# Five of ten down-weight pieces built behind the next tile's gate operands in a SwiGLU layer

## Chip, cores and metric

The kernel runs one whole transformer layer on one core of a Trainium2 chip, as one launch. The metric is device time in microseconds (us) of that launch, as the median of several runs. TensorE is called PE here (its weight loads PEld), VectorE DVE, ScalarE ACT, GpSimd POOL and SyncE SP; SP issues the DMA transfers that are spoken of below.

## What is computed

The layer has a mixer (a Fourier part and a retention part) and a SwiGLU channel mixer. The change is in the second one. Cut to it, the reference is:

```python
def swiglu(u, wg, wu, wd):
    return (jax.nn.silu(u @ wg) * (u @ wu)) @ wd

u2 = modulate(layer_norm(x), sh2, sc2)          # (1, 2048, 1024)
x = layer_norm(DEEPNORM_ALPHA * x + gt2 * swiglu(u2, w_ffn_gate[l], w_ffn_up[l], w_ffn_down[l]),
               ln2_g[l], ln2_b[l])              # gate, up: 1024 x 2816, down: 2816 x 1024
```

All of it is in float32. The kernel makes each float32 operand of a product into two float16 parts (high and low) and multiplies three pairs of them, so one product costs three passes of PE.

## The kernel before

**Tiles.** The 2816 hidden columns are cut into 22 blocks of 128, taken two at a time: `j` runs over `HJ` = 11 tiles, and for each `j` the loop `for gu` does the gate (`gu` = 0) and then the up projection (`gu` = 1). Below, G3 is the gate half of tile 3 and U3 its up half. Each half is one level of a Strassen scheme: seven products of half-size operands instead of eight, for each of the two halves of the sequence (`sb` 0 and 1). So a half is 14 products, and a product is 12 matmuls of 128x128 by 128x512 (`prod`, with the three passes of `mm3`, L152 to L154).

**PSUM banks.** A sequence half uses one bank `x` (`proj` for `sb` 0, `misc` for `sb` 1), into which A11, S2, S3 (and A22) are summed one onto the other, and one bank `z` (`s0`, `s1`) for S1 and S4. A12 has a bank of its own (`tq`, `zt`). After A11, S2 and S3 the present sum is copied out by ACT into a tile named `p`, `a` or `b` (`keep`, L1353). PE may add the next product onto `x` only when this copy is done. The order of the products in a half is A11 S1 (`sb` 0), A11 S1 (`sb` 1), S2, S2, then A12 S3, A12 S3, then A22 S4, A22 S4. `done` finishes a quarter: DVE adds (L1340 of the gate, L1347 and L1348 or L1344 of the up), ACT applies silu (L1338, L1341). After an up quarter, `h_part` makes sums of the hidden tile on POOL (L1306 to L1314), splits some in two with ACT and DVE (`half_split` into the tile `ht`, of which there is one, L1187 and L1188), and SP stores them.

**Operands.** For each half, SP loads two raw weight tiles (`w_raws`, L1104). `right` makes seven operands of them: POOL does four subtractions (L985, L987, L990, L992), and `split` makes the float16 parts into `ws` tiles, high on ACT (L148), low on DVE (L149). This runs one half ahead of PE.

**Down weights.** The second matrix product, with `w_ffn_down`, comes later and reads operands from DRAM. They are made in the loop over `j`, in ten pieces, `down(i, c)` with `i` from 0 to 4 and `c` 0 or 1; below D0 to D9 in the order of their issue. A piece loads two raw tiles in four transfers (L1199), has POOL scale them by the output gate (L1200) and form differences (L1213 to L1216 and L1225 to L1228, 24 instructions), has ACT and DVE split 17 groups of them into `wdo` tiles (L148, L149; there are two such tiles), and has SP store seven results (L1210, L1221). The eleventh tile has a different function, `down_last`.

**What sets the order.** Every engine runs its instructions in program order. The order within an engine comes from a scheduler that simulates the program when it is built; it takes the source order as priority and places an instruction of later source where an engine would stand idle in its simulation. Tiles come from pools by tag: three `raw` tiles are shared by gate, up and down weights, twelve `ws` tiles by operands and temporaries. So a piece's loads can only start when a raw tile of the stream ahead of it is free, and the next gate's or up's load only when the piece has let go of one.

In source order the program makes the operands of G0, U0, D0, G1, U1, D1, G2 and so on; with the half ahead, the work of D(n) in the trace lies beside PE's G(n).

Of the kernel before, what the change touches and what calls it, by code (L numbers as in the profile page):

```python
# [79 lines left out]
def layer_kernel(ctx: ExitStack, tc: tile.TileContext, a, out):  # L80
# [19 lines left out]
    def mk(pool, shape, dt=F32, tag=None, bufs=1):  # L100
        return pool.tile(shape, dt, name=nm(tag), tag=tag, bufs=bufs)
# [26 lines left out]
    def raw_tile(shape=(P, 2, 512), dt=F32):  # L128
        return mk(wp, list(shape), dt, tag="raw", bufs=3)

    def ws_tile(shape=(P, 2, 512), dt=F16):
        return mk(wp, list(shape), dt, tag="ws", bufs=12)
# [14 lines left out]
    def split(hi, lo, raw, scale=SW):  # L147
        S.activation(hi, raw, AF.Copy, scale=scale)  # L148
        V.scalar_tensor_tensor(lo, raw, scale, hi, ALU.mult, ALU.subtract)  # L149
# [1024 lines left out]
    HP = HJ // 2  # L1174
# [15 lines left out]
    def down(i, c):  # L1190

        raws = []
        for half in range(2):
            raw = raw_tile((P, 2, 4, P))
            r0 = (2 * i + HJ * half) * P
            gv = gt2.rearrange("p (q n) -> p q n", q=4)[:, :, c * P : (c + 1) * P]
            for k in range(2):
                src = wd_in[r0 + k * P : r0 + (k + 1) * P].rearrange("p (q n) -> p q n", q=4)
                Q.dma_start(raw[:, k], src[:, :, c * P : (c + 1) * P])  # L1199
                G.tensor_tensor(raw[:, k], raw[:, k], gv, ALU.mult)  # L1200
            raws.append(raw)
        q0, q1 = raws[0][:, :, 0:2], raws[0][:, :, 2:4]
        q2, q3 = raws[1][:, :, 0:2], raws[1][:, :, 2:4]
        t1 = ws_tile((P, 2, 2, P), F32)

        def op(o, x):
            if o in ONE:
                w = mk(cq, [P, 2, 2, 2, P], F16, tag="wdo", bufs=2)
                split(w[:, :, 0], w[:, :, 1], x)
                Q.dma_start(wd_d[o][:, 2 * i : 2 * i + 2, c], w.rearrange("p k s y n -> p k s (y n)"))  # L1210
                return
            t = ws_tile((P, 4, P), F32)
            G.tensor_tensor(t[:, 3], x[:, 0, 1], x[:, 0, 0], ALU.subtract)  # L1213
            G.tensor_tensor(t[:, 0], x[:, 1, 1], t[:, 3], ALU.subtract)
            G.tensor_tensor(t[:, 1], x[:, 1, 1], x[:, 0, 1], ALU.subtract)
            G.tensor_tensor(t[:, 2], x[:, 1, 0], t[:, 0], ALU.subtract)  # L1216
            w = mk(cq, [P, 7, 2, P], F16, tag="wdo", bufs=2)
            split(w[:, 0:2, 0], w[:, 0:2, 1], x[:, :, 0])
            split(w[:, 2:6, 0], w[:, 2:6, 1], t)
            split(w[:, 6, 0], w[:, 6, 1], x[:, 1, 1])  # L1220
            Q.dma_start(wd_d[o][:, :, i, c], w)  # L1221

        op(0, q0)
        op(1, q2)
        G.tensor_tensor(q0, q1, q0, ALU.subtract)  # L1225
        G.tensor_tensor(t1, q3, q0, ALU.subtract)
        G.tensor_tensor(q1, q3, q1, ALU.subtract)
        G.tensor_tensor(q2, q2, t1, ALU.subtract)  # L1228
        for o, x in enumerate((t1, q1, q2, q0, q3)):
            op(2 + o, x)  # L1230
# [49 lines left out]
    for j in range(HJ):  # L1280
# [37 lines left out]
        for gu, src in enumerate((wg_in, wu_in)):  # L1318
# [44 lines left out]
            def product(o, sb, loose=False):  # L1363


                d = st[sb]
                if o == A11:
                    d["x"] = prod(w, o, sb, (("proj", "misc")[sb],))
                    keep(sb, "p", d["x"])
                elif o == A12:  # L1370
                    done(sb, 0, d["p"], prod(w, o, sb, (("tq", "zt")[sb],)))
                elif o == S2:
                    keep(sb, "a", prod(w, o, sb, None, d["x"]))
                elif o == S1:
                    d["z"] = prod(w, o, sb, (("s0", "s1")[sb],))
                elif o == S3:
                    keep(sb, "b", prod(w, o, sb, None, d["x"]))
                    done(sb, 3, d["b"], d["z"])
                elif o == A22 and loose:
                    done(sb, 2, d["b"], prod(w, o, sb, (("tq", "zt")[sb],)))  # L1380
                elif o == A22:
                    done(sb, 2, None, prod(w, o, sb, None, d["x"]))
                else:
                    done(sb, 1, d["a"], prod(w, o, sb, None, d["z"]))
# [18 lines left out]
            else:  # L1403

                for part in (ORDER[0:2], ORDER[2:3], ORDER[3:5], ORDER[5:7]):
                    for sb in range(2):
                        for o in part:
                            product(o, sb)
        if j < 2 * HP:
            down(j // 2, j % 2)  # L1410
    es_c.close()


# [103 lines left out]
    for o, sb in TWO:  # L1517
        hq, last = h_next
        n = TWO.index((o, sb)) + 1
# [163 lines left out]
```

## Time and profile before

| | |
|---|---|
| three runs | 2118.32 us median (2117.81 to 2122.67) |
| the profiled execution | 2121.23 us, of it a span of 2119.4 us |
| PE busy in the span | 2025.6 us (96%) |
| DVE busy | 1408.6 us (66%) |
| ACT busy | 795.0 us (38%) |
| POOL busy | 757.0 us (36%) |

The times in the trace are counted from the start of the span. The loop over `j` has its gate half G1 at about 993 us and then a half every 36.26 us where PE does not wait. In a row of a timeline, the two numbers ahead are start and duration; brackets give how long the engine stood idle before and what released it. A row of the waits gives the sum, the count and the longest. A row of the windows gives, after the stretch and its length, the busy time of PE, PEld, DVE, ACT and POOL with the number of instructions in brackets, then PE's granted clock, the DMA share and GB/s.

### The profile page before, as it was taken

What the parts mean: (1) busy time and instruction counts of PE and PEld (TensorE: products, weight loads), DVE (VectorE), ACT (ScalarE), POOL (GpSimd) and SP (SyncE); (2) the same over time, 40 slices, a digit from 0 to 9 for tenths busy, and PEclk for the clock granted to TensorE, in tenths of its full rate; (3) what the DMA queues carried; (4) which work ended last, traced back from release to release, by engine and by line L of the source; (5) the groups of instructions that cost most, each with busy time, mean ns of one, the idle gap of its engine ahead of it and who ended that gap; (6) DMA issues with size and microseconds to landing.
All of it is one profiled execution on the core that took longest, in us unless ns stands there. A gap on an engine that the chain in (4) does not pass through costs nothing.

```text
span 2119.4 us, 30963 instructions
## 1 busy us (share of the span) xinstructions
PE 2025.6 (96%) x11678; PEld 1178.6 (56%) x11678; DVE 1408.6 (66%) x2546; ACT 795.0 (38%) x1438; POOL 757.0 (36%) x800
## 2 busy tenths in 40 slices
PE   6999989999999899989899999999999999999997
PEld 5456676458557544444344444444444458888743
DVE  7976385757547577786566556656655558878676
ACT  5624432243233244463433443343334324333132
POOL 3322412221222136646675566556655500000010
PEclk9999999999999999999999999999999999999999
DMA  9531121332211545644434443444444369665652
GB/s 292 179 120 51 37 63 60 110 96 64 89 45 51 168 166 194 229 139 148 138 121 142 123 144 127 141 123 146 129 126 143 115 235 346 208 221 204 245 179 105
DMA packets 300342, 305.19 MB, mean 144 GB/s; under 512 B 15448, under 2 KB 248992, under 8 KB 299040
## 3 DMA queue, kind: packets, MB, share of 16 engines
q1 hardware_dynamic: 293376, 287.08, 42.3%
q10 hardware_dynamic: 6816, 16.12, 2.1%
q8 instruction: 92, 1.51, 0.3%
q14 instruction: 58, 0.48, 0.1%
HBM read 200.25 MB, written 102.90 MB: 143 GB/s over the span
## 4 chain that ended last, share of the span: by engine, by line
PE 57%; DVE 17%; DMA 9%; POOL 8%; ACT 4%; issue 3%; SPq 2%; POOLq 0%; DVEq 0%; ACTq 0%
PE proj L152 8%; PE proj L154 8%; PE proj L153 8%; PE misc L152 4%; PE misc L154 4%; PE misc L153 4%; PE s L152 3%; PE s L154 3%; PE s L153 3%; DMA raw<-in_w_mod_dram 3%; DVE raw L377 2%; DVE ws L149 2%; DMA raw<-in_w_ffn_down_dram 1%; DVE st L178 1%; POOL us L1088 1%
## 5 line engine op out<-in xcount | busy, mean ns | idle before, releaser
L152 PE MATMUL proj<-ws,uhi 128*128 128x512 f16 (+1 forms) x768 | 251.2, 327 | 4.2 <-ACT sg L774 3.2
L154 PE MATMUL proj<-ws,ulo 128*128 128x512 f16 (+1 forms) x768 | 251.1, 327 | 0.0
L153 PE MATMUL proj<-ws,uhi 128*128 128x512 f16 (+1 forms) x768 | 251.0, 327 | 0.0
L153 PEld LDWEIGHTS <-ws 128*128 128x128 f16 x1296 | 127.8, 99 | 172.7 <-issue 25.4
L152 PEld LDWEIGHTS <-ws 128*128 128x128 f16 x1296 | 127.7, 99 | 155.8 <-issue 6.8
L154 PEld LDWEIGHTS <-ws 128*128 128x128 f16 x1296 | 127.4, 98 | 153.6 <-issue 3.2
L167 POOL TENSOR_TENSOR rstd<-ve,mhalf 128x1 f32<-128x1 f32 x66 | 38.9, 599 | 455.6 <-DVE ve L165 444.0
L149 DVE SCALAR_TENSOR_TENSOR ws<-raw,ws 128x512 f16<-128x512 f32 x186 | 146.0, 800 | 62.8 <-ACT ws L148 61.0
L148 ACT ACTIVATE ws<-raw 128x512 f16<-128x512 f32 x186 | 114.0, 626 | 89.1 <-POOL raw L992 40.8
L1187 ACT CAST ho<-h 128x1280 f16<-128x1280 f32 x70 | 87.4, 1258 | 151.9 <-DVE h L1440 35.7
L149 DVE SCALAR_TENSOR_TENSOR wdo<-raw,wdo 128x256 f16<-128x256 f32 (+1 forms) x100 | 66.5, 687 | 109.1 <-ACT wdo L148 109.1
L152 PE MATMUL proj<-u2b,ws 128*128 128x512 f16 x344 | 130.8, 380 | 8.4 <-ACT a L1353 4.0
L152 PE MATMUL misc<-u2a,ws 128*128 128x512 f16 x344 | 130.2, 379 | 6.6 <-ACT p L1353 4.7
L154 PE MATMUL proj<-u2b,ws 128*128 128x512 f16 x344 | 131.1, 381 | 0.0
L153 PE MATMUL proj<-u2b,ws 128*128 128x512 f16 x344 | 130.9, 380 | 0.0
L153 PE MATMUL misc<-u2a,ws 128*128 128x512 f16 x344 | 130.4, 379 | 0.1
L154 PE MATMUL misc<-u2a,ws 128*128 128x512 f16 x344 | 130.4, 379 | 0.0
L1188 DVE TENSOR_TENSOR ho<-h,ho 128x1280 f16<-128x1280 f32 x70 | 103.9, 1489 | 20.2 <-ACT ho L1187 20.1
L153 PEld LDWEIGHTS <-uhi 128*128 128x128 f16 x768 | 75.5, 98 | 46.9 <-issue 5.3
L154 PEld LDWEIGHTS <-ulo 128*128 128x128 f16 x768 | 75.6, 98 | 44.8
L152 PEld LDWEIGHTS <-uhi 128*128 128x128 f16 x768 | 76.0, 99 | 42.9 <-issue 1.3
L149 DVE SCALAR_TENSOR_TENSOR wdo<-ws,wdo 128x512 f16<-128x512 f32 (+2 forms) x70 | 58.7, 861 | 50.4 <-ACT wdo L148 49.4
(493 smaller groups left out, 5304.5 us busy)
## 6 DMA issues: line engine op xcount, KB each, us to landing
h<-h SPq DMA_DIRECT2D x40, 640.0 KB
raw<-in_w_mod_dram SPq DMA_DIRECT2D x88, 256.0 KB
wd<-wdo SPq DMA_DIRECT2D x50, 448.0 KB
wd<-wd SPq DMA_DIRECT2D x33, 640.0 KB
h<-sg SPq DMA_DIRECT2D x60, 256.0 KB
raw<-in_w_ffn_gate_dram SPq DMA_DIRECT2D x22, 512.0 KB
raw<-in_w_ffn_up_dram SPq DMA_DIRECT2D x22, 512.0 KB
raw<-in_w_ffn_down_dram SPq DMA_DIRECT2D x40, 256.0 KB
```

The costliest lines, as they stand in the source:

```text
L148: S.activation(hi, raw, AF.Copy, scale=scale)
L149: V.scalar_tensor_tensor(lo, raw, scale, hi, ALU.mult, ALU.subtract)
L152: T.matmul(o, sh, mh, start=first, stop=False, skip_group_check=onto)
L153: T.matmul(o, sh, ml, start=False, stop=False, skip_group_check=onto)
L154: T.matmul(o, sl, mh, start=False, stop=last, skip_group_check=onto)
L167: pows.append(G.tensor_tensor(rstd, ve, mhalf[:, 0:n], ALU.pow).ins)
L178: V.bn_stats(st[:, hf], xt[:, hf * 512 : hf * 512 + 512])
L377: V.scalar_tensor_tensor(r[0], r[k], sil[:, v, k : k + 1], r[0], ALU.mult, ALU.add)
L1088: (V if o in (2, 5) or (sb and i >= 2 and o != 4) else G).tensor_tensor(dst[:, :, 1], src, dst[:, :, 0], ALU.subtract)
L1187: S.copy(dst[:, 0], src)
L1188: V.tensor_tensor(dst[:, 1], src, dst[:, 0], ALU.subtract)
```

## The change

The call of `down` goes into the loop over gate and up. Piece n = j - 1 of the first five is issued behind the gate of tile j, so behind the gate that follows its old place; pieces five to nine stay behind the up of their own tile.

```diff
@@ -1406,8 +1406,10 @@
                     for sb in range(2):
                         for o in part:
                             product(o, sb)
-        if j < 2 * HP:
-            down(j // 2, j % 2)
+
+            n = j - 1 if gu == 0 else j
+            if (gu == 0 and 0 <= n < HP) or (gu == 1 and HP <= n < 2 * HP):
+                down(n // 2, n % 2)
     es_c.close()
```

The source order was U0 D0 G1 U1 D1 G2 U2 D2 G3 ... and is now U0 G1 D0 U1 G2 D1 U2 G3 D2 U3 G4 D3 U4 G5 D4 U5 D5 G6; from G6 on both are alike. No instruction is added or taken away in `down` itself.

The first place is POOL's order behind the operands of U0 (`ws_9737` is a temporary of theirs). Before, the four scalings L1200 of D0 (`raw_10005`, `raw_10010`) and its differences follow at once:

```order
L987 TENSOR_TENSOR ws_9737<-raw_9735,raw_9733 128x512
L1200 TENSOR_TENSOR raw_10005<-raw_10005,gt_9623 128x512 x2
L992 TENSOR_TENSOR raw_9735<-raw_9735,ws_9737 128x512
L1213 TENSOR_TENSOR ws_10016<-raw_10005 128x128
L1215 TENSOR_TENSOR ws_10016<-raw_10005 128x128
L1214 TENSOR_TENSOR ws_10016<-raw_10005,ws_10016 128x128
L1200 TENSOR_TENSOR raw_10010<-raw_10010,gt_9623 128x512
```

Now the operands of G1 (`raw_10007`, `raw_10009`, L985 to L992) come first, and D0 (now `raw_10237`, `raw_10242`) after and between them:

```order
L987 TENSOR_TENSOR ws_9737<-raw_9735,raw_9733 128x512
L992 TENSOR_TENSOR raw_9735<-raw_9735,ws_9737 128x512
L985 TENSOR_TENSOR raw_10007<-raw_10007 128x512
L1200 TENSOR_TENSOR raw_10237<-raw_10237,gt_9623 128x512
L990 TENSOR_TENSOR raw_10007<-raw_10009,raw_10007 128x512
L987 TENSOR_TENSOR ws_10011<-raw_10009,raw_10007 128x512
L1200 TENSOR_TENSOR raw_10237<-raw_10237,gt_9623 128x512
L992 TENSOR_TENSOR raw_10009<-raw_10009,ws_10011 128x512
L1200 TENSOR_TENSOR raw_10242<-raw_10242,gt_9623 128x512 x2
L1213 TENSOR_TENSOR ws_10248<-raw_10237 128x128
```

D0 has moved behind one whole set of operands, that of G1.

The second place is ACT's order while PE does G2. The tiles `p_`, `a_`, `b_` are the copies out of the banks `proj` and `misc`; the `wdo` rows are the first splits of a down piece, of its scaled raw tile. Before, they stand ahead of the copies `a`:

```order
L1187 CAST ht_10593<-sg_10094 128x512
L1353 COPY p_10758<-misc_10745 128x512
L148 ACTIVATE ws_10941<-raw_10919 128x512
L148 ACTIVATE wdo_11218<-raw_11194 128x2x128
L148 ACTIVATE wdo_11218<-raw_11194 128x128
L148 ACTIVATE ws_10944<-raw_10919 128x512
L1353 COPY a_10785<-proj_10717 128x512
L1353 COPY a_10799<-misc_10745 128x512
L148 ACTIVATE wdo_11205<-ws_11200 128x4x128
L1341 ACTIVATE sg_10685<-sg_10685 128x512
L1353 COPY b_10828<-proj_10717 128x512
```

Now the copies `a` come first, and the first splits of the down piece stand ahead of the copies `b`:

```order
L148 ACTIVATE ws_10937<-raw_10917 128x512
L148 ACTIVATE ws_10941<-raw_10919 128x512
L1187 CAST ht_10593<-sg_10006 128x512
L148 ACTIVATE ws_10944<-raw_10919 128x512
L1353 COPY a_10697<-proj_10629 128x512
L1353 COPY a_10711<-misc_10657 128x512
L148 ACTIVATE ws_11196<-raw_11191 128x512
L148 ACTIVATE wdo_11437<-raw_11421 128x2x128
L148 ACTIVATE wdo_11437<-raw_11421 128x128
L1341 ACTIVATE sg_10597<-sg_10597 128x512
L1353 COPY b_10740<-proj_10629 128x512
```

The wait for a piece's raw tile has moved from the copy of the second product onto `proj` to that of the third, and the splits of the up operands (`raw_10919`) stand among the rows ahead of `a`.

The third place is SP's order around the raw tiles of U2 (`raw_10917`, `raw_10919`). Before, both are loaded together, behind the last store of D1:

```order
L1221 DMA wd_9615<-wdo_10669 896x1x256
L1210 DMA wd_9616<-wdo_10677 128x2x512
L1104 DMA raw_10689<-in_w_ffn_gate_dram 128x8x128
L1210 DMA wd_9617<-wdo_10681 128x2x512
L1104 DMA raw_10917<-in_w_ffn_up_dram 128x8x128
L1104 DMA raw_10919<-in_w_ffn_up_dram 128x8x128
```

Now the second one stands alone, behind a store of D1 and stores of the hidden tile:

```order
L1293 DMA h_9584<-sg_10005 256x1x256
L1293 DMA h_9585<-hs_10522 256x1x256
L1210 DMA wd_9616<-wdo_10909 128x2x512
L1104 DMA raw_10919<-in_w_ffn_up_dram 128x8x128
L1221 DMA wd_9615<-wdo_10901 896x1x256
```

The first load `raw_10917` has stayed far ahead; the second one now follows the piece that holds the third raw tile.

## Prediction

> **What bounds the kernel now.** I read the page first, then the waits of PE, then the windows of the stretch that the change touches.
>
> ```profile
> span 2119.4 us, 30963 instructions
> PE 2025.6 (96%) x11678; PEld 1178.6 (56%) x11678; DVE 1408.6 (66%) x2546; ACT 795.0 (38%) x1438; POOL 757.0 (36%) x800
> ```
>
> PE is busy 96% of the span. The change gives PE no work and takes none, so it can only move PE's waits, and only where it moves instructions, from U0 to G5. The windows show this stretch by halves and tiles; the second number is the length, the third is PE's busy time.
>
> ```profile
> 937.90:975.10 37.20, 35.82 (x165) 15.99 (x165) 25.73 (x35) 20.18 (x42) 27.60 (x32) 1.00 0.28 79
> 975.10:992.80 17.70, 16.71 (x76) 7.42 (x76) 12.31 (x19) 6.66 (x12) 4.21 (x4) 1.00 0.65 193
> 1100.00:1172.00 72.00, 72.00 (x335) 32.59 (x333) 43.55 (x55) 27.63 (x55) 43.55 (x44) 1.00 0.44 133
> ```
>
> From 1100 us on PE is full: there is nothing to win there. What there is to win lies before it, and the waits of PE name it (from 940 to 1100 us, then from 1100 to 1690 us):
>
> ```profile
> PE misc L152 <- ACT p L1353: 3.6, 2, 3.3
> PE proj L152 <- ACT a L1353: 3.5, 2, 2.1
> PE s L152 <- DVE sg L1340: 1.3, 1, 1.3
> PE proj L152 <- ACT p L1353: 0.9, 1, 0.9
> PE s L152 <- DVE c L1347: 0.7, 1, 0.7
> PE misc L152 <- ACT b L1353: 0.3, 1, 0.3
> ```
>
> ```profile
> PE misc L152 <- ACT p L1353: 1.2, 3, 0.7
> PE proj L152 <- ACT a L1353: 0.6, 1, 0.6
> ```
>
> The first list sums to 10.3 us: U0 has 1.3 + 0.7 + 0.3 = 2.3, G2 has 0.3 + 1.3 = 1.6 (its parts of the first two rows), and G1 has the rest, 0.9 + 3.3 + 2.1 = 6.3. G1 also pays for a low clock right behind its longest wait:
>
> ```profile
> 1018.86:1022.27 3.41, 3.41 (x10) 1.20 (x9) 1.72 (x3) 1.15 (x2) 3.17 (x4) 0.50 0.21 77
> ```
>
> 3.41 us at a granted clock of 0.50 do the work of 1.7 us, so 1.7 us are lost and G1 costs 8.0 in all. **The stake is 2.3 + 8.0 + 1.6 = 11.9 us**, half a per cent of the time. After 1100 us all waits sum to 1.8 us, most of them in tiles that the change leaves alone.
>
> The waits of G1 come from ACT's queue, not from its load; here are its rows in that stretch:
>
> ```profile
> 1003.13 0.61 ACT L148 ACTIVATE wdo<-raw 128x256 f16<-128x256 f32 x2 [1.75 <-POOL raw L1200]
> 1003.66 0.57 ACT L1353 COPY p<-proj 128x512 f32<-128x512 f32 x1
> 1009.15 0.63 ACT L148 ACTIVATE ws<-raw 128x512 f16<-128x512 f32 x1 [4.93 <-POOL raw L992]
> 1009.69 0.57 ACT L1353 COPY p<-misc 128x512 f32<-128x512 f32 x1
> 1016.61 0.62 ACT L1187 CAST ht<-hs 128x512 f16<-128x512 f32 x1 [4.79 <-DMA h<-ht]
> 1017.14 0.58 ACT L1353 COPY a<-proj 128x512 f32<-128x512 f32 x1
> ```
>
> Each copy that PE wants stands behind an instruction that itself waits: for a down piece (L1200), for POOL's last operand of the next up half (L992), for the store of `ht`.
>
> **The change, part by part.** *U0.* D0's splits leave PE's way there. The add that PE waited for sat on DVE behind one of them:
>
> ```profile
> 974.02 0.43 DVE L149 SCALAR_TENSOR_TENSOR wdo<-raw,wdo 128x256 f16<-128x256 f32 x1 [1.32 <-ACT wdo L148]
> 974.36 0.68 DVE L1340 TENSOR_TENSOR sg<-a,s 128x512 f32<-128x512 f32 x1
> ```
>
> Of 2.3 I leave 0.5 (bounds 0 and 2.3): -1.8.
>
> *G1.* D1 no longer stands ahead of `p<-proj`, so the wait of 0.9 goes. L992 and the store of `ht` remain ahead of the next two copies, and D0, which now runs from U0's late products into G1, takes D1's place on POOL. Floor: two thirds of the 6.3 gone, 2. Ceiling: all as now, 8. The two waits left sum to 3.3 + 2.1 = 5.4; with a difference of D1 less ahead of each on POOL (0.46, the row of L1213 below) they come to 4.5, and the longer, 2.8, is shorter than the 3.3 behind which the low clock stood. I take 4.5: -3.5.
>
> *G2 to G4.* Here the change can lose. The present state, in G3, which begins at 1148.42 us:
>
> ```profile
> 1164.97 0.62 ACT L148 ACTIVATE wdo<-raw 128x256 f16<-128x256 f32 x2 [3.91 <-POOL raw L1200]
> 1165.49 0.61 ACT L148 ACTIVATE ws<-raw 128x512 f16<-128x512 f32 x1
> 1166.01 0.56 ACT L1353 COPY a<-proj 128x512 f32<-128x512 f32 x1
> ```
>
> ```profile
> 1161.37 0.38 PE L152 MATMUL misc<-u2a,ws 128*128 128x512 f16 x1
> 1163.96 0.38 PE L152 MATMUL tq<-u2b,ws 128*128 128x512 f16 x1
> 1166.62 0.38 PE L152 MATMUL proj<-u2b,ws 128*128 128x512 f16 x1
> ```
>
> A product takes 1163.96 - 1161.37 = 2.59 us. The copy ends at 1166.57, PE uses it at 1166.62: the slack of `a<-proj` is 0.05 us already. The order shows that the piece's first split moves from ahead of `a<-proj` (needed by the 8th product) to ahead of `b<-proj` (needed by the 11th), three products or 7.8 us later. But the piece is later too. I rebuild its chain from the durations of the old one:
>
> ```profile
> 1092.31 0.46 POOL L1213 TENSOR_TENSOR ws<-raw 128x128 f32<-128x128 f32 x1
> 1121.03 1.26 POOL L987 TENSOR_TENSOR ws<-raw,raw 128x512 f32<-128x512 f32 x1 [8.70 <-DMA raw<-in_w_ffn_gate_dram]
> 1162.44 2.49 POOL L1200 TENSOR_TENSOR raw<-raw,gt 128x512 f32<-128x512 f32 x2 [4.02 <-DMA raw<-in_w_ffn_down_dram]
> ```
>
> ```profile
> 1116.23 0.64 SPq L1104 DMA_DIRECT2D raw<-in_w_ffn_gate_dram  x1
> 1159.00 1.27 SPq L1199 DMA_DIRECT2D raw<-in_w_ffn_down_dram  x2
> ```
>
> ```profile
> 1129.11 0.69 DVE L149 SCALAR_TENSOR_TENSOR ws<-raw,ws 128x512 f16<-128x512 f32 x1 [0.71 <-ACT ws L148]
> ```
>
> From a piece's first L1213 to the load into the raw tile that it frees: 1116.23 - 1092.31 = 23.9. From that load to L987: 1121.03 - 1116.23 = 4.8. From L987 to the last split of the set: 1129.80 - 1121.03 = 8.8. From a down load to L1200: 1162.44 - 1159.00 = 3.4, and L1200 takes 2.5. In the new order a piece's L1213 needs a `ws` tile that the 6th product of the up half lets go: 6 x 2.59 = 15.5 us into it, or 20.7 us before the next gate. So, from the gate's start: second up load at +3.2, L987 at +8.0, last split and with it the next down loads at +16.8, L1200 at +20.2, done +22.7. Then ACT's `wdo` split (0.62) and DVE's part behind it with an add, a silu and the copy `b<-proj` (0.56, as `a`): some 3.7 in sum, so +26.4. PE needs it after ten products, at +25.9: **0.5 us late**, if nothing else holds the chain up.
>
> What may hold it up is that the piece now meets the up half's own DVE work. The up half has less of POOL's, the gate half more:
>
> ```profile
> 1112.16:1148.42 36.26, 36.26 (x169) 16.43 (x168) 20.39 (x28) 12.72 (x25) 14.73 (x12) 1.00 0.44 132
> 1148.42:1184.68 36.26, 36.26 (x169) 16.46 (x168) 23.17 (x28) 15.24 (x30) 28.98 (x33) 1.00 0.44 135
> ```
>
> so 14 us of POOL's time change halves and the load is evener, if anything. But a multiply of the up takes longer when POOL works (here beside L1308) than when it doesn't:
>
> ```profile
> 1137.60 0.69 DVE L1348 SCALAR_TENSOR_TENSOR sg<-c,sg 128x512 f32<-128x512 f32 x1
> 1146.90 1.75 DVE L1348 SCALAR_TENSOR_TENSOR sg<-c,sg 128x512 f32<-128x512 f32 x1
> ```
>
> That is 1.06 us each. Two such steps inside the chain, and sums of `h` between the piece's steps on POOL (1.3 to 1.7 us each), give a late copy of up to 4 to 5 us; nothing in the way gives 0. I take the value near the lower middle, 0.5 + 1.06 + about half a sum = 2 in each of G2, G3 and G4. The Trainium skill (SBUF — State Buffer, "Who interferes with whom") says that a DVE instruction with two SBUF inputs contends with a GpSimd instruction that reads SBUF, and that the loser waits for the whole instruction. The 1.75 against 0.69 agrees in kind; by that rule every multiply that meets a piece would pay, which speaks for the upper end and against the change, and the sum would be nearer 4 than 2 per gate.
>
> *G5.* The last moved piece, D4, is done in U5 and D5 follows at its old place, so `a<-misc` stands behind a later L1200: 0.6 to 3, taken as 2. *G6 on*: same order, nothing.
>
> *The DMAs.* A piece's four loads and seven stores move with it, on the same queue and in the same number; at a DMA share of 0.44 I give them nothing, and the second up load that slips behind them is in the chain above.
>
> **Sum.** Before 2.3 + 8.0 + 1.6 = 11.9. After 0.5 + 4.5 + 3 x 2 + 2 = 13.0. That is +1.1 on the profiled execution's 2121.2 us. The profile lies 2.9 us above the median of the runs, which is 2118.3, so I forecast **2119.4 us**: no change. A measurement of this kernel tells about 0.3%, 6.4 us, from none. With the small ends (0, 2, 0, 0, 0, 0.6) the sum is 2.6, with the large ones 2.3 + 8 + 3 x 4.5 + 3 = 26.8: from -9.3 to +14.9.
>
> **Rivals.**
> *A: the moved pieces fit.* The slack of three products is enough in G2 to G5 and only G1 keeps 2 to 3 us. For it: the load gets evener, and the chain above is late by 0.5 only. Against it: `a<-proj` and `p<-misc` had hardly any slack before. Sum 2.6 instead of 11.9: 2109.
> *B: the third product becomes the wait of every gate, slower.* `b<-proj` at 11 products, late by 4 to 5 us in each of G2 to G5, since multiplies and sums of `h` lengthen the piece; G1 as now, 8. It decides as soon as the chain grows by over 3 us from +26.4. From 3.3 us on, such a wait would bring the low clock too, 1.7 us each. 0.5 + 8 + 4 x 4.5 = 26.5, or +14.6: 2133; with the low clock four times 2140. The Trainium skill (TensorE: Matmul & The Clock Gate, Part 1, "What's actually happening") gives an idle window of about 3.4 us as what halves the clock; G1's low clock stood behind 3.28 us, and by that figure a wait of 2 stays free of it.
> *C: the change doesn't do what it says.* The `raw` and `ws` tiles hold a piece back anyway, so that it runs where it ran, and only the queues differ: within 2 us, 2118.
>
> **Chances.** Forecast 0.48, A 0.25, B 0.22, C 0.05. Most of A, all beyond -6.4, is faster: 0.24 with a bit of the forecast's lower side. B nearly all is slower, with some of the forecast's upper side: 0.25. The rest, 0.51, is within 0.3%. The range takes A's 2109 and B's 2133 as ends, without B's low clock; the likeliest case alone, 2113 to 2125.
>
> **What the profile after would show.** Right: the waits on `p` and `a` of G1 shrink to 4 to 5 us with no low clock; U0 loses its wait on `sg`; in G2 to G4 the waits name `b` with about 2 us, behind a `wdo` split released by L1200. A: no waits from 1045 us on. B: `b` with 4 us or more in each gate, and a granted clock under 1 in that stretch. Wrong in another way: waits that name PE's weights (`ws`), since then the second up load, not ACT's queue, would be what is late; or a wait in an up half, which I have as free.

## The result

| | before | after |
|---|---|---|
| median, us | 2120.49 (4 runs, 2117.81 to 2125.43) | 2147.15 (4 runs, 2142.49 to 2151.64) |
| ratio to before | | 1.0118, 95% interval 1.0096 to 1.0140 |
| span of the profiled execution, us | 2119.4 | 2147.9 |

The kernel became slower by 1.2%, some 25 us. The forecast was no change, and the time lies above the range that was given. The profile of the changed kernel answers to the first two lines shown in the prediction:

```profile
span 2147.9 us, 30963 instructions
PE 2033.2 (95%) x11678; PEld 1178.3 (55%) x11678; DVE 1421.7 (66%) x2546; ACT 798.7 (37%) x1438; POOL 767.9 (36%) x800
```

The same number of instructions is busy longer on PE (by 7.6 us) and on DVE (by 13.1 us). To see where the time came from, both executions are cut at the same points of the program: the first of the last seven products of G0, A12 onto `tq` in U1, and A12 onto `tq` in G6. The windows of the kernel before:

```profile
937.91:1053.12 115.21, 106.50 (x481) 47.31 (x480) 75.97 (x96) 51.31 (x103) 76.84 (x79) 0.99 0.43 127
1053.12:1381.65 328.53, 326.90 (x1514) 147.96 (x1512) 200.76 (x248) 122.24 (x240) 196.66 (x192) 1.00 0.44 134
```

and of the kernel after:

```profile
936.28:1045.83 109.55, 105.84 (x481) 47.20 (x481) 64.53 (x85) 47.44 (x92) 60.51 (x55) 0.98 0.35 103
1045.83:1406.64 360.81, 336.70 (x1514) 149.74 (x1513) 223.49 (x259) 129.39 (x250) 222.33 (x215) 0.98 0.43 131
```

The start (U0, G1 and the first part of U1) gained 115.21 - 109.55 = 5.7 us. The stretch of the moved pieces D1 to D4 behind it lost 360.81 - 328.53 = 32.3 us. Of the remaining program, the part ahead took 1.6 us less and the part behind 3.5 us more. Of the 32.3 us, 9.8 are the same 1514 matmuls taking longer (336.70 against 326.90). Some 8 of these are the low clock: in five places, behind waits that end at 1084.96, 1102.52, 1167.45, 1262.25 and 1326.85 us, the granted clock over the next 3.41 us is 0.50 to 0.59. The rest of the 32.3 us is PE standing still. The waits of PE name the places; first from 936 to 1046 us, then from there to 1407 us:

```profile
PE proj L152 <- ACT a L1353: 2.8, 1, 2.8
PE misc L152 <- ACT u2a L1087: 1.6, 1, 1.6
PE misc L152 <- ACT p L1353: 0.6, 1, 0.6
PE proj L152 <- ACT b L1353: 0.3, 1, 0.3
```

```profile
PE misc L152 <- ACT p L1353: 13.2, 6, 3.4
PE proj L152 <- ACT b L1353: 6.8, 3, 2.8
PE s L152 <- DVE c L1347: 2.3, 4, 1.8
PE misc L152 <- ACT b L1353: 1.7, 1, 1.7
```

Each of the four gates G2 to G5 waits about 3 us (2.8 to 3.4) for the copy `p` of `misc` and then 1.5 to 2.8 us for a copy `b`; G2 also waits 1.8 us for an add of the up half before it. The forecast had the wait on `b`, at 2 us, and had nothing for the one on `p`.

**The copy `b`.** Its chain can be followed step by step as it was rebuilt in the prediction, here from D2 in U2 over the second up load and the first down load of D3 to PE's product in G3. POOL, SP and PE of the kernel after:

```profile
1130.08 0.46 POOL L1213 TENSOR_TENSOR ws<-raw 128x128 f32<-128x128 f32 x1 [4.70 <-PE misc L154]
1161.28 1.27 POOL L987 TENSOR_TENSOR ws<-raw,raw 128x512 f32<-128x512 f32 x1 [0.45 <-DMA raw<-in_w_ffn_up_dram]
1176.40 2.49 POOL L1200 TENSOR_TENSOR raw<-raw,gt 128x512 f32<-128x512 f32 x2 [7.18 <-DMA raw<-in_w_ffn_down_dram]
```

```profile
1156.80 0.65 SPq L1104 DMA_DIRECT2D raw<-in_w_ffn_up_dram  x1
1173.06 26.62 SPq L1199 DMA_DIRECT2D raw<-in_w_ffn_down_dram  x4
```

```profile
1183.45 0.38 PE L152 MATMUL proj<-u2b,ws 128*128 128x512 f16 x1 [1.51 <-ACT b L1353]
```

The piece takes 1156.80 - 1130.08 = 26.7 us (rebuilt: 23.9), its load to L987 4.5 (4.8), from there to the next down load 11.8 (8.8), to L1200 3.3 (3.4), and from there to PE's product 7.1 (6.2). That is 53.4 us where 47.1 were forecast. PE needs 18 products, 46.6 us, between the two ends, so along this chain a tile loses 6.8 us, however that is shared out between the waits and the low clock.

**The copy `p`.** It stands on ACT behind a cast into the one tile `ht`, which waits for the store of the part before:

```profile
1155.84 0.62 ACT L1187 CAST ht<-sg 128x512 f16<-128x512 f32 x1 [0.54 <-POOL sg L1314]
...
1165.26 0.62 ACT L1187 CAST ht<-hs 128x512 f16<-128x512 f32 x1 [5.42 <-DMA h<-ht]
1165.79 0.62 ACT L148 ACTIVATE ws<-ws 128x512 f16<-128x512 f32 x1
1166.32 0.61 ACT L148 ACTIVATE ws<-raw 128x512 f16<-128x512 f32 x1
1166.84 0.56 ACT L1353 COPY p<-misc 128x512 f32<-128x512 f32 x1
```

That store was late because DVE had not made the low part of `ht`. DVE of the same kernel:

```profile
1158.54 1.16 DVE L149 SCALAR_TENSOR_TENSOR wdo<-ws,wdo 128x512 f16<-128x512 f32 x1
1159.62 1.75 DVE L1348 SCALAR_TENSOR_TENSOR sg<-c,sg 128x512 f32<-128x512 f32 x1
1161.30 1.79 DVE L1188 TENSOR_TENSOR ht<-sg,ht 128x512 f16<-128x512 f32 x1
1163.02 1.75 DVE L149 SCALAR_TENSOR_TENSOR wdo<-raw,wdo 128x512 f16<-128x512 f32 x1
```

The cast of 1155.84 had its DVE part L1188 only at 1161.30. Between the two, DVE's queue held a low part of the next gate's operands, an add, a low part of the moved piece and a multiply. The windows from six products behind the A12 of U2, some 5 us before the gate, to the sixth product of G3 show it; DVE's time is the third pair, POOL's the fifth. Before:

```profile
1143.24:1161.37 18.13, 18.13 (x85) 8.23 (x84) 14.99 (x15) 5.76 (x10) 13.81 (x9) 1.00 0.51 171
```

and after:

```profile
1145.38:1167.45 22.07, 18.45 (x85) 8.22 (x84) 20.92 (x20) 8.18 (x16) 20.05 (x16) 0.99 0.69 211
```

DVE had 3.1 us to spare in this stretch before (14.99 of 18.13). Now DVE and POOL are both nearly full, 20.92 and 20.05 of 22.07 us. Most of DVE's growth here is number: 20 instructions in place of 15, at a mean of 1.05 us in place of 1.00. Over the whole tile, low parts became longer, too. One tile of the kernel before, and then of the kernel after, with the mean in ns behind the busy time:

```profile
L149 DVE SCALAR_TENSOR_TENSOR ws<-raw,ws 128x512 f16<-128x512 f32 x14 | 10.7, 779 | 5.1 <-ACT ws L148 5.0
L149 DVE SCALAR_TENSOR_TENSOR wdo<-raw,wdo 128x256 f16<-128x256 f32 (+2 forms) x10 | 6.6, 679 | 12.5 <-ACT wdo L148 12.5
```

```profile
L149 DVE SCALAR_TENSOR_TENSOR ws<-raw,ws 128x512 f16<-128x512 f32 x12 | 11.6, 964 | 8.6 <-ACT ws L148 8.4
L149 DVE SCALAR_TENSOR_TENSOR wdo<-raw,wdo 128x256 f16<-128x256 f32 (+2 forms) x10 | 9.9, 1021 | 7.0 <-ACT wdo L148 7.0
```

The ten low parts that DVE makes from a piece's raw tiles take 9.9 us in place of 6.6, with the same shapes. Not every group grew: the mean of the multiplies L1348 fell from 1128 to 1070 ns. In sum DVE is busy 47.7 us in this tile in place of 43.8.

### The profile page after: what moved, and what is told of

It is laid out like the page before. It is cut to its first block, busy times and chain, and to the rows that moved or that the text cites. A ratio compares the mean times of both kernels' runs of the same rounds, so it can differ in the third digit from the quotient of the medians.

```text
span 2147.9 us, 30963 instructions
## 1 busy us (share of the span) xinstructions
PE 2033.2 (95%) x11678; PEld 1178.3 (55%) x11678; DVE 1421.7 (66%) x2546; ACT 798.7 (37%) x1438; POOL 767.9 (36%) x800
## 4 chain that ended last, share of the span: by engine, by line
PE 47%; DVE 22%; DMA 11%; POOL 9%; ACT 4%; issue 4%; SPq 1%; DVEq 0%; POOLq 0%; ACTq 0%
PE proj L152 7%; PE proj L154 7%; PE proj L153 7%; PE misc L152 3%; PE misc L154 3%; DMA raw<-in_w_mod_dram 3%; PE misc L153 3%; PE s L152 3%; PE s L153 3%; PE s L154 3%; DVE wdo L149 3%; DVE raw L377 2%; DVE ws L149 2%; DMA raw<-in_w_ffn_down_dram 2%; DVE sg L1348 2%
## 5 line engine op out<-in xcount | busy, mean ns | idle before, releaser
L149 DVE SCALAR_TENSOR_TENSOR ws<-raw,ws 128x512 f16<-128x512 f32 x186 | 153.5, 838 | 88.0 <-ACT ws L148 86.3
L152 PE MATMUL misc<-u2a,ws 128*128 128x512 f16 x344 | 132.3, 385 | 18.0 <-ACT p L1353 14.7
L152 PE MATMUL proj<-u2b,ws 128*128 128x512 f16 x344 | 132.5, 385 | 12.2 <-ACT b L1353 7.1
L149 DVE SCALAR_TENSOR_TENSOR wdo<-raw,wdo 128x256 f16<-128x256 f32 (+1 forms) x100 | 75.9, 787 | 86.9 <-ACT wdo L148 86.9
L153 PE MATMUL proj<-u2b,ws 128*128 128x512 f16 x344 | 132.7, 386 | 0.0
L154 PE MATMUL proj<-u2b,ws 128*128 128x512 f16 x344 | 132.6, 385 | 0.0
L153 PE MATMUL misc<-u2a,ws 128*128 128x512 f16 x344 | 132.2, 384 | 0.1
L154 PE MATMUL misc<-u2a,ws 128*128 128x512 f16 x344 | 132.1, 384 | 0.0
L1188 DVE TENSOR_TENSOR ho<-h,ho 128x1280 f16<-128x1280 f32 x70 | 103.8, 1488 | 21.2 <-ACT ho L1187 21.1
L149 DVE SCALAR_TENSOR_TENSOR wdo<-ws,wdo 128x512 f16<-128x512 f32 (+2 forms) x70 | 64.0, 936 | 54.0 <-ACT wdo L148 53.2
```

The costliest lines, as they stand in the source:

```text
L152: T.matmul(o, sh, mh, start=first, stop=False, skip_group_check=onto)
L153: T.matmul(o, sh, ml, start=False, stop=False, skip_group_check=onto)
L154: T.matmul(o, sl, mh, start=False, stop=last, skip_group_check=onto)
L1188: V.tensor_tensor(dst[:, 1], src, dst[:, 0], ALU.subtract)
```

## Experiments

Four theories of the cause stood after the result: the shared raw tiles (the chain of `b`), the one `ht` (the chain of `p`), DVE being overloaded at the new place, and lateness as such. Ratios are to the kernel before, with 95% intervals.

| run | edit | median, us | ratio |
|---|---|---|---|
| e1 | only D0 moved | 2127.1 | 1.0014 (1.0001 to 1.0028) |
| e2 | only D1 to D4 moved | 2149.7 | 1.0123 (1.0105 to 1.0142) |
| e3 | after, two `ht` | 2152.3 | 1.0127 (1.0099 to 1.0155) |
| e4 | after, no low parts of moved pieces | 2117.3 | 0.9972 (0.9962 to 0.9983) |
| e5 | after, own raw tile | 2145.6 | 1.0116 (1.0097 to 1.0136) |
| e6 | before, own raw tile | 2121.8 | 1.0004 (0.9994 to 1.0015) |
| e7 | before, no low parts of these pieces | 2115.4 | 0.9981 (0.9964 to 0.9998) |
| e8 | before, two `ht` | 2127.3 | 1.0030 (1.0018 to 1.0041) |
| e9 | after, own raw tile and two `ht` | 2146.5 | 1.0128 (1.0111 to 1.0145) |
| e10 | only D0 moved, own raw tile | 2123.8 | 1.0014 (1.0005 to 1.0023) |
| e11 | all pieces a whole tile later | 2120.3 | 0.9996 (0.9986 to 1.0005) |
| e12 | only D0 moved, own raw tile and two `ht` | 2127.1 | 1.0031 (1.0017 to 1.0044) |
| e13 | after, no differences of moved pieces | 2132.3 | 1.0041 (1.0026 to 1.0056) |
| e14 | as e11, D8 and D9 both behind U9 | 2127.0 | 1.0020 (1.0009 to 1.0032) |

### Which pieces lose: e1 and e2

```diff
 # e1
-            if (gu == 0 and 0 <= n < HP) or (gu == 1 and HP <= n < 2 * HP):
+            if (gu == 0 and 0 <= n < 1) or (gu == 1 and 1 <= n < 2 * HP):
 # e2
+            if (gu == 0 and 1 <= n < HP) or (gu == 1 and (n == 0 or HP <= n < 2 * HP)):
```

> Only D0 is moved behind G1; D1 to D9 stay where they were before. Theory 1 (the gain of the change sits in U0 and G1, the loss in every later moved piece): the wait of U0 on the add of the gate goes and G1's waits fall as they did in the changed kernel (9 us of waits and low clock before, 4 after), while G2 to G5 keep the waits of before (under 2 us); 2120 less about 6, so 2112 to 2116. Rival (moving D0 alone pushes D0 and D1 into one another, since D1 then follows with one half less between them): G1 and U1 lose what U0 wins, 2118 to 2128.

> D1 to D4 are moved, D0 stays. Theory 1: U0 and G1 as before (no gain), G2 to G5 as in the changed kernel, each gate with a wait of about 3 us on the copy p of misc and 1.5 to 2.8 on the copy b, with low clock behind the first: 2120 plus about 32, so 2148 to 2156. Rival (the loss is a consequence of D0's shift that runs on from tile to tile): under 2135.

The whole loss is in D1 to D4: e2 is as slow as the change. Moving D0 alone won nothing. U0 and G1 gained, as in the changed kernel, but D1 follows D0 there by half a tile, and the waits from 936 to 1100 us show how it was given back. The rows of `b` and `sg` lie at the end of G1 and the start of U1, and 2.5 us of the row of `a` in U1:

```profile
PE proj L152 <- ACT a L1353: 6.0, 3, 2.8
PE misc L152 <- ACT b L1353: 1.6, 1, 1.6
PE s L152 <- DVE sg L1340: 1.6, 1, 1.6
```

So the time fits the rival for e1, and theory 1 for e2.

### The one `ht` and the raw tiles: e3, e5 and e9

```diff
 # e3: one c instead of two makes room
-                ht = mk(cq, [P, 2, 512], F16, tag="ht", bufs=1)
+                ht = mk(cq, [P, 2, 512], F16, tag="ht", bufs=2)
 # e5: c is written into its summand to make room
-            raw = raw_tile((P, 2, 4, P))
+            raw = raw_tile((P, 2, 4, P)) if half else mk(cq, [P, 2, 4, P], tag="rawd", bufs=1)
 # e9: the edits of e3 and e5, c as in e5, with p and b sharing three tiles
```

> The changed kernel with two ht tiles instead of one (and, to make room, one c tile instead of two, which only DVE writes and reads). Theory A (p of misc is late because it stands on ACT behind a cast into the one ht, which waits for DVE's split and the store of the part before): the wait of about 3.2 us on p and the low clock behind it go from G2 to G5, b stays or grows, since PE no longer gives it time: 2147 less 4 x 3 to 5, so 2127 to 2136. Rival B (the second up load is late and the splits of the up operands ahead of p would hold it anyway): p keeps over 2 us in each gate, 2142 or more.

> The changed kernel, in which the first of a piece's two raw tiles comes from a place of its own (room for it: the sum c of L1347 is written into its summand, so the c tiles go). Theory L (the loss is a closed loop: PE's sixth product of an up half, the piece, the raw tile that it frees, the second up load, its splits, the next piece's load and scaling, the copy b, PE; about 53 us where PE's 18 products between these points take 46.6): with a fourth raw tile the second up load no longer waits for the piece, the loop is open, and the waits of G2 to G5 fall below 2 us each: 2147 less 20 to 32, so 2115 to 2127. Rival D (DVE alone, loaded beyond what fits between the up's adds, whoever holds the raw tiles): the wait on p stays at 2 to 3 us with its low clock, 2138 or more.

> The changed kernel with both: a raw tile of its own for a piece, as in e5_own_raw, and two ht tiles (room for them: c written into its summand, p and b share three tiles). Two-cause theory (p late over the one ht, b late over the shared raw tiles; each alone leaves the other, which takes up what the first lets go): both waits go, G2 to G5 lose under 2 us each, and the gain in U0 and G1 stays: 2112 to 2125. Rival (DVE's backlog of some 20 us around each change from up to gate holds PE by some other copy or add whatever the tiles): a wait of 3 us or more with low clock stays in each gate, 2135 or more.

The time fits rival B of e3, rival D of e5 and the rival of e9. The waits tell more. From 1070 to 1400 us, the two largest rows of e3:

```profile
PE proj L152 <- ACT b L1353: 12.0, 3, 4.1
PE proj L152 <- ACT a L1353: 8.0, 4, 5.3
```

of e5:

```profile
PE misc L152 <- ACT p L1353: 14.9, 5, 3.4
PE s L152 <- DVE a L1347: 2.5, 4, 1.9
```

and of e9:

```profile
PE proj L152 <- ACT a L1353: 14.5, 4, 3.6
PE misc L152 <- ACT pb L1353: 2.4, 6, 1.4
```

With two `ht` the wait on `p` falls from 3.4 to at most 0.8 us, as theory A had it, and other copies take its place: `b` with 4 us in G2 to G4, `a` with 5.3 us in G5. With an own raw tile the wait on `b` falls to at most 0.7 us, and `p` keeps 3.4 us in every gate. With both, PE waits 3.6 us in every gate on a third copy, `a`, which stands on ACT behind splits that wait for POOL's L992; in G3 that one comes behind a scaling and sums of `h` and then waits 0.6 us for a low part. From 1158.0 to 1171.7 us, the stretch up to its end, DVE is busy all of the 13.7 us and POOL 13.1 of them. Each chain was real, and neither was the cause by itself: taking away a link moved the wait to the next copy.

### DVE at the new place: e4 and e7

```diff
+    split0, half0 = split, lambda hi, lo, raw: (S.activation(hi, raw, AF.Copy, scale=SW), V.memset(lo, 0.0))
     def down(i, c):
+        split = half0 if 2 * i + c < HP else split0
```

> The changed kernel, in which the five moved pieces leave out the low parts of their operands: DVE sets them to zero instead of computing them, so the second matrix product is computed with less exact weights. All else stays: loads, POOL's work, ACT's high parts, stores. Theory A1 (DVE is the one that is overloaded where the up's adds and hidden-tile splits meet the piece's low parts, and the delay reaches p over ht): the wait on p falls under 1 us in G2 to G5 and the low clock goes: 2118 to 2130. Rival A2 (the serial chain of cast, split and store of the one ht is too long by itself) or B (the late second up load): p keeps over 2 us, 2138 or more.

> The kernel before, in which the first five pieces leave out the low parts of their operands (zeros from DVE), as in e4_no_low. It gives what these parts cost at the old place: G2 to G5 have no waits there, so only U0 and G1 can gain, up to 10 us: 2111 to 2119. If the place alone made no difference to DVE, it would gain as much as the changed kernel did, about 30: 2090 to 2095.

Here the loss is gone (2117.3 us, 0.7 below the range expected for it). Of the changed kernel with DVE's low parts left out and short writes of zeros in their place, the waits from 1070 to 1400 us are

```profile
PE misc L152 <- ACT p L1353: 1.9, 2, 1.6
PE misc L152 <- ACT b L1353: 1.5, 1, 1.5
PE proj L152 <- ACT a L1353: 0.6, 1, 0.6
PE proj L152 <- ACT b L1353: 0.2, 1, 0.2
```

Leaving the same work out saves 30 us at the new place (2147.2 to 2117.3) and some 5 at the old one (e7). Without DVE's share the two placements can't be told apart, 0.9972 and 0.9981 with overlapping intervals. In the window that answers to the two above, e4 (1134.64 to 1152.77 us) has POOL as full as the changed kernel, 17.97 of 18.13 us, but DVE at 12.06, and PE doesn't wait. So the loss needs DVE's low parts at this place; the loads, the stores, POOL's and ACT's work without them don't bring it.

### Too many instructions, or longer ones: e13

```diff
     def down(i, c):
+        sub_ = (lambda o, *r: G.memset(o, 0.0)) if 2 * i + c < HP else G.tensor_tensor
...
-        G.tensor_tensor(q0, q1, q0, ALU.subtract)
+        sub_(q0, q1, q0, ALU.subtract)      # and the seven other lines of this kind
```

> The changed kernel, in which the five moved pieces leave out their differences: POOL writes zeros over the results of L1213 to L1216 and L1225 to L1228 instead of reading and subtracting (the second product is computed with these weights missing). DVE's low parts are all there. If DVE's own work at this place is too much as it is (its instructions at the length they have beside an idle POOL, 0.69 for 128x512): the waits stay, 2138 or more. If it is the stretch of DVE's instructions while POOL reads and works (1.0 to 1.75 for the same shapes): the instructions of DVE in the piece's stretch come down to about 0.7, the backlog goes and G2 to G5 lose under 2 us each, 2113 to 2125. In between, if only the sums of h (L1306 to L1314) still stretch them: 2125 to 2138.

The time lies between the two. With POOL's differences left out and every DVE instruction kept, the loss falls from 25 to about 10 us. In the window that answers to the two above DVE is no longer full:

```profile
1144.25:1164.28 20.03, 18.30 (x86) 8.23 (x84) 14.06 (x16) 5.85 (x12) 15.30 (x11) 1.00 0.73 226
```

So more than half of the loss needs POOL's differences beside DVE's low parts. The run doesn't tell number from length: DVE has fewer instructions in this window (16 for 20), and they are shorter (0.88 us for 1.05 in the mean). Nor is a full DVE all there is to it, since some 10 us are lost with DVE at 14.06 us in this window, less than in the kernel before (14.99). The waits that are left from 1070 to 1400 us (8.4 us on `p` in five, 5.7 on `b` of `proj` in four) come with ACT's casts behind the store of `ht`, up to 6.7 us in the one place looked at. What holds that store stays open; the profiled execution took 2140.4 us, where the median is 2132.3.

### Placement or lateness: e11 and e14

```diff
 # e11, against the changed kernel
-            n = j - 1 if gu == 0 else j
-            if (gu == 0 and 0 <= n < HP) or (gu == 1 and HP <= n < 2 * HP):
+            n = j - 1
+            if 0 <= n < 2 * HP and gu == (n < 2 * HP - 1):
 # e14: D8 and D9 behind the up of tile 9
```

> All pieces one whole tile later instead of half a tile: D0 to D8 behind the up of tiles 1 to 9, at the place in the tile where the kernel before has them, D9 behind the gate of tile 10. Theory (what loses is the place within the tile, in the up half, not the lateness): no waits in G2 to G9; the start has one piece less: 2108 to 2117, or up to 2124 if D9, half a tile behind D8, costs like a moved piece. Rival (lateness itself costs): 2130 or more.

> As e11_tile_later, with D8 and D9 both behind the up of tile 9. In e11 the tiles G1 to G10 had no wait over 0.5 us, and U10 lost 9 us, where D9 came half a tile behind D8. If D9 right behind D8 fits there: 2107 to 2115. If two pieces in one tile cost as they did there (9 us or more) wherever they are: 2116 to 2124.

A whole tile later costs nothing in the tiles between: from 960 to 1600 us e11's PE waits 0.6 us in all,

```profile
PE misc L152 <- ACT p L1353: 0.4, 1, 0.4
PE proj L152 <- ACT a L1353: 0.2, 1, 0.2
```

and it comes to G10 14.3 us ahead of the kernel before, counted from the first cut in each (937.91 us before, 937.06 here). It gives 8.2 us of that back up to the seventh product of G10. From 1600 to 1700 us it waits mostly at the start of G10 (not in U10, as the expectation of e14 has it), where D9, behind a gate, has the place of the moved pieces and follows D8 by half a tile:

```profile
PE s L152 <- DVE c L1347: 4.9, 2, 3.6
PE misc L152 <- ACT p L1353: 1.3, 1, 1.3
PE proj L152 <- ACT a L1353: 0.5, 1, 0.5
```

Its median is that of the kernel before, though the execution profiled here took 4.7 us less than that median, so where the longer ones lose time isn't known. Putting D9 right behind D8 (e14) made the end worse, with waits up to 3.7 us there and a time above both ranges that were expected. So lateness is not what costs, up to a whole tile. The place within the tile does, and e1 and e14 suggest that two pieces close together do as well.

### The tiles without the change: e6, e8, e10 and e12

The edits of e5, e3 and e9 in the kernel before (e6, e8), or with D0 alone moved (e10, e12).

> The kernel before with the same tile of its own for a piece. Theory L: G2 to G5 have no waits to win, so only U0 and G1 (11 us) can change: 2112 to 2121. Rival (the earlier loads of the pieces crowd the queues): 2123 or more.

> The kernel before with two ht tiles (and one c tile). The wait of 2.1 us on a in G1, behind the store of ht, goes, and perhaps part of the 3.3 us on p: 2114 to 2119. Rival (as in the changed kernel, the wait only moves to the next copy of the same gate): 2118 to 2123.

> Only D0 moved, with the raw tile of its own. In e1_d0_only U0 and G1 gained, and U1 and G2 gave it back by waits on b, on the add of the gate and on a, since D1 follows D0 by half a tile there. If that is the shared raw tile: 2112 to 2118. If it is the work itself (two pieces in one tile on POOL and DVE): 2118 to 2126.

> Only D0 moved, with the raw tile of its own and two ht tiles. If both tiles are what crowds U1 and G2 behind D0: 2108 to 2115. If POOL's and DVE's work is: 2117 to 2126.

None of them won, and e8 and e12 came out above both of their ranges. In e6 PE had no wait from 1050 us to the last up half, but there a wait of 4.0 us came in with the edit, which makes `c` a `ws` tile in that half. In e10 and e12 the crowd behind D0 stayed, so the shared tiles are not what holds it there. That the work of two pieces in one tile does is what is left, and was not tested by itself. In e8 the waits of G1 stayed (3.3 us on `p`, 2.0 on `a`), and the two `ht` with one `c` made the kernel before slower by 0.3%; why was not followed up. No version was found that beats the kernel before with the whole work done.

## Why the prediction was wrong

- **U0** (2.3 us to 0.5): right, and a little better. No wait of U0 is left in the kernel after.
- **G1** (8.0 to 4.5): near in sum, and partly by luck. The wait of 0.9 us on `p` of `proj` went, as forecast. Of the other two, the wait on `p` of `misc` fell from 3.3 to 0.6 us and the one on `a` grew from 2.1 to 2.8, where both were to shrink by 0.46. With 0.3 us on `b` that is 3.7 us. A low clock, which the forecast had excluded, stands behind the wait of 2.8 us (0.55 over the 3.41 us from 1010.19), so G1 costs some 5.2. The start gained 5.7 us where 5.3 were forecast.
- **G2 to G4 at 2 us each, G5 at 2**: this is the step that failed. The stretch lost 32 us, not 6. The sum held only the wait on `b`. That wait came to 6.8 + 1.7 = 8.5 us in the four gates, near the 8 of the sum, but this is luck: along the chain 6.8 us a tile were late, not 0.5 to 2, and the waits on `p` ahead took up most of it (in e3, where `p` hardly waits, `b` waits 4 us). The chain was the right one; its steps were taken from places where DVE had room, and two of them came out 3 us longer. What the sum put at nothing is the larger part: the waits on `p`, 13.2 us in the stretch, though the prediction says under rival A that this copy "had hardly any slack"; the low clock behind waits on `p` and `b`, some 8 us; and 2.3 us on `c`. As e3, e5 and e9 show, repairing one copy's wait would not have given the time, since the waits on `p` and `b` come from one crowd on DVE and POOL.
- **"The load is evener, if anything"**: this sentence let the large values go. It compares POOL's time in whole halves of 36 us. The crowd is some 20 us long and lies across the border of two halves, and it is DVE's as much as POOL's: 3.1 us of DVE were free there, and the moved piece brings its low parts. Over a whole tile DVE is busy only 60% (43.55 of 72.00 in the prediction's row).
- **The low clock.** The prediction put G1's low clock down to the wait of 3.3 us and took waits of 2 to 2.8 us as free of it. That was a misreading, and it took the low clock out of the sum. In the kernel before, the clock behind the wait of 3.3 us (which ends at 1010.31) is full, and it is low behind the wait of 2.1 us (which ends at 1017.76):

```profile
1010.31:1013.72 3.41, 3.41 (x16) 1.56 (x16) 3.41 (x3) 1.51 (x3) 3.30 (x3) 1.00 0.39 105
1017.76:1021.17 3.41, 3.40 (x11) 1.36 (x11) 1.72 (x4) 1.87 (x5) 3.17 (x5) 0.66 0.41 138
```

  In the kernel after, the clock is low behind waits of 2.8 and 2.5 us and full behind one of 3.1 us (ending at 1102.52, 1262.25 and 1246.62):

```profile
1102.52:1105.93 3.41, 3.41 (x10) 1.26 (x10) 2.50 (x4) 2.14 (x4) 0.00 (x0) 0.57 0.00 0
1262.25:1265.66 3.41, 3.41 (x9) 1.30 (x9) 2.49 (x4) 2.14 (x4) 0.00 (x0) 0.53 0.00 0
1246.62:1250.03 3.41, 3.41 (x16) 1.56 (x16) 1.59 (x4) 1.27 (x3) 1.58 (x1) 1.00 0.84 272
```

  The Trainium skill (TensorE: Matmul & The Clock Gate, Part 1, "What's actually happening") says that the clock falls after an idle window of about 3.4 us, and that this window is free-running. That it runs freely agrees with these rows, in which the place of a wait matters and not its length alone; a whole idle window was not needed, since 2.1 us were enough here.
- **Rival B** had the right sign, the right gates and the low clock; its price without that clock, 2133, and with it, 2140, was nearest. It named only `b`, though, at 4 to 5 us, where `b` waited 1.5 to 2.8 us and `p` about 3. **Rival A** (the pieces fit) and **C** (nothing moves) fell.
- **DVE beside POOL.** The Trainium skill (SBUF — State Buffer, "Who interferes with whom") says that a DVE instruction with two SBUF inputs contends with a GpSimd instruction that reads SBUF. By it the prediction had nearer 4 us a gate, and it did not follow that. The rows agree: in the tile shown, DVE's low parts from a piece's raw tiles grew by half (679 to 1021 ns), while in the same crowd the adds and multiplies that take one input from a PSUM bank (L1347, L1344) kept 0.67 to 0.68 us. Putting POOL's writes of zeros in place of its differences (e13) took more than half of the loss away.

## What to carry to other kernels

Before work is moved on a side engine, look at that engine's busy time in windows as short as the moved work, across the borders of stages: an engine that is busy 60% of a tile can be at 83% for the 18 us that matter (14.99 of 18.13) and have too little room. Where PE waits behind queues that full engines feed, a further buffer may only move the wait to the next copy, as it did here three times; a run that leaves out one engine's work shows which engine it is. A chain rebuilt from durations measured where the engines have room comes out too short (47.1 against 53.4 us here), and a slack of less than 1 us should be given a term of its own in the sum.

## What was not expected of the hardware

The low clock came behind waits of 2.1, 2.5 and 2.8 us and not behind two of 3.1 and 3.3 us, as shown above, so the length of a wait alone didn't decide it. The price was large: some 8 us of the 32 us that the stretch lost are matmuls at the low clock. And two engines slow one another: of POOL's 128x512 subtractions, L992 at 1195.51 us, where DVE is idle, took 1.27 us and L990 at 1162.50, in the crowd, 1.71; DVE's low parts of that shape took 0.69 us at 1185.34, where POOL is idle, and up to 1.75 in the crowd.
